# Rotating a batch of images by 180 degrees: the first store's lead strip in five transfers instead of one

## The chip, the cores and the metric

The kernel runs on one core of one Trainium2 chip. The metric is the time of one execution on the device in microseconds (us); a smaller number is better. Three executions of the kernel before gave 121.90, 121.97 and 122.13 us, median 121.97.

## The reference

The input is 32 x 3 images of 256 x 256 float32 values, 25.2 MB. Each image is turned by 180 degrees, which reverses its 65536 values when it is read as one row:

```python
def setup_inputs():
    batch, c, h, w = 32, 3, 256, 256
    return {"x": np.random.randn(batch, c, h, w).astype(np.float32)}

def reference(x: np.ndarray) -> np.ndarray:
    return np.rot90(x, k=2, axes=(-2, -1)).astype(np.float32)
```

## The kernel before

Nothing is computed; data is moved and reversed. Each of the 96 images is cut into four quarters of E = 16384 values (64 KB). A quarter is one partition's row in SBUF. The 384 quarters are three groups of 128: A holds the even ones of the first 64 images (image quarters 0 and 2), Bt the odd ones of the same images, Ct all four quarters of the last 32 images. All three tiles are in SBUF at once.

Reversing an image is done in two parts. The order of the quarters is turned by the store: the destination access pattern walks an image's quarters backwards (`::-1` in `store`, lines 52 to 54), so a store of group A names 64 images with 2 quarters each, in reversed order. The values within a quarter are turned in place by VectorE (DVE): `swap` (lines 56 to 60) exchanges a block of up to J = 2048 columns at the left with its mirror block at the right, with three reversing copies through a scratch tile T. `turn` (lines 69 to 73) does this for a stretch of left columns; a whole tile takes four swaps of 2048, 12 copies.

The work stands in the program in this order:

- loads (lines 64 to 67): A on SP's DMA queue, Bt on ACT's queue, behind it in the source Ct on SP's queue. Line 65 is a small memset that delays Bt's load. SP's queue is q1 in the profile, ACT's is q10. All stores go out on SP's queue too. Each DMA is spread over the 16 DMA engines, and in each engine the transfers of one queue run in the order of their issue; the last thing that an engine does for a transfer is a 4-byte write to a semaphore, here called the completion write. The transfer has landed when all 16 counts are there.
- line 76 turns the outer three blocks of A (columns 0 to 6143 and their mirrors); line 77 stores the first LEAD = 256 columns of A, 1 KB of each of 128 partitions. This is the strip. It is final as soon as the first swap is done.
- line 78 turns part of Bt, line 79 the innermost block of A, line 80 stores the rest of A (columns 256 to 16383, 63 KB a partition), called A's big store.
- lines 81 and 82: the rest of Bt and its store; lines 83 and 84: Ct and its store.

The strip waits for A's first swap and A's load alone, so SP issues it early, long before A's big store, and it stands in q1 behind C's load, which is still running. DVE's instructions are kept in program order (line 47). SP's instructions stand in the order of the source, each with a wait for what it needs; at the end of the program SP waits for the semaphore of every DMA, four instructions of at most two conditions each, then drains and meets the other engines at a barrier. DMA semaphores are handed out in turn from eight.

Of the kernel before, what the change touches and what calls it, by code (L numbers as in the profile page):

```python
# [2 lines left out]

os.environ.setdefault("NEURON_RT_ULTRASERVER_MODE", "4")

# [4 lines left out]


@with_exitstack
def kernel(
    ctx: ExitStack,
    tc: tile.TileContext,
    x: bass.AP,
    out: bass.AP,
):
    nc = tc.nc  # L20
    P = 128

    B, C, H, W = x.shape
    L = H * W
    G = 32
    E = L // 4
    J = E // 8

    xr = x.rearrange("b c h w -> (b c) (h w)").rearrange(
        "m (s e) -> (m s) e", s=4)  # L30
    om = out.rearrange("b c h w -> (b c) (h w)").rearrange(
        "m (s e) -> m s e", s=4)
    rows = 2 * P
    x4 = [xr[0:rows:2], xr[1:rows:2], xr[rows:rows + P]]
    o4 = [om[0:2 * G, 1::2], om[0:2 * G, 0::2], om[2 * G:3 * G]]

    pool = ctx.enter_context(tc.tile_pool(name="slots", bufs=1))
    A = pool.tile([P, E], x.dtype, tag="A")
    Bt = pool.tile([P, E], x.dtype, tag="B")
    Ct = pool.tile([P, E], x.dtype, tag="C")  # L40
    T = pool.tile([P, J], x.dtype, tag="T")

    def back(t, lo, hi):
        return t[:, hi - 1:(lo - 1 if lo else None):-1]

    def copy(dst, src):
        tc.keep_in_program_order(nc.vector.tensor_copy(out=dst, in_=src))  # L47

    def load(t, g, lo, hi, queue=nc.sync):
        return queue.dma_start(out=t[:, lo:hi], in_=x4[g][:, lo:hi])  # L50

    def store(t, g, lo, hi):
        return nc.sync.dma_start(
            out=o4[g][:, ::-1, lo:hi], in_=t[:, lo:hi])

    def swap(t, lo, w):
        hi = E - lo - w
        copy(T[:, 0:w], back(t, hi, hi + w))
        copy(t[:, hi:hi + w], back(t, lo, lo + w))
        copy(t[:, lo:lo + w], T[:, 0:w])  # L60

    MID = 2560
    LEAD = 256
    load(A, 0, 0, E)
    nc.vector.memset(Bt[:, 0:256], 0.0)  # L65
    load(Bt, 1, 0, E, nc.scalar)
    load(Ct, 2, 0, E)

    def turn(t, lo, hi):
        while lo < hi:  # L70
            w = min(J, hi - lo)
            swap(t, lo, w)
            lo += w

    half = E // 2
    turn(A, 0, half - J)
    store(A, 0, 0, LEAD)
    turn(Bt, 0, MID)
    turn(A, half - J, half)
    store(A, 0, LEAD, E)  # L80
    turn(Bt, MID, half)
    store(Bt, 1, 0, E)
    turn(Ct, 0, half)
    store(Ct, 2, 0, E)


# [1 line left out]
_INS = ['x']  # L88
_OUTS = [((32, 3, 256, 256), 'float32')]


# [23 lines left out]
```

## Time and profile before

| | |
|---|---|
| median of three executions | 121.97 us (121.90 to 122.13) |
| the profiled execution's own time | 121.90 us |
| its span, first to last instruction | 120.12 us |
| A's load landed | 39.45 us |
| Bt's load landed | 44.28 us |
| C's load landed, on the first and the last DMA engine | 60.72 and 61.23 us |
| strip: issued, landed on the last engine | 43.25 and 61.60 us |
| A's big store: issued, landed | 59.76 and 80.62 us |
| Bt's store: issued, landed | 70.31 and 99.96 us |
| C's store: issued, landed | 85.45 and 119.33 us |
| DVE busy | 44.9 us, 40 instructions |

The profile is of one execution. Its times count from the first instruction. A DMA instruction of SP or ACT is only the issue, some 0.4 to 0.6 us; the data moves later, in packets, one for each row of a transfer (64 KB, 63 KB or 1 KB here) and one for each completion write. The trace has each packet's start, length, size and queue, not its DMA engine. An engine starts its next packet about 4 ns before the last one ends. GB/s and DMA share count a packet in the slice in which it starts, so short slices can show more than the engines can carry.

### The profile page before, as it was taken

The numbers are of one execution on the slowest core, as the hardware profiler recorded it, in microseconds if no ns is written. First come the engines' busy times: TensorE is split into PE (matmuls) and PEld (weight loads), VectorE is DVE, ScalarE is ACT, GpSimd is POOL, SyncE is SP. The second block draws the span as 40 slices with busy tenths as digits, with TensorE's granted clock in tenths as the row PEclk, the third lists the DMA queues.
The fourth block names the chain that finished last, engine by engine and source line by source line (L and its number), as shares of the span: only waits on it lengthen the run. The fifth ranks groups of instructions, "written<-read, shape, count | busy, mean of one in ns | idle before, by whom it ended". The sixth has DMA issues, their size and how long they took to land.

```text
span 120.1 us, 97 instructions
## 1 busy us (share of the span) xinstructions
DVE 44.9 (37%) x40; POOL 0.2 (0%) x4
## 2 busy tenths in 40 slices
DVE  0000000000000899999999999999400000000000
POOL 0000000000000000000000000000000000000000
DMA  9888988898889988998899777988898889888980
GB/s 349 349 349 371 677 349 349 349 698 349 349 349 633 415 349 349 546 502 349 349 387 687 344 344 344 687 349 349 349 698 349 349 349 698 349 349 349 677 371 0
DMA packets 1008, 50.33 MB, mean 419 GB/s; under 512 B 112, under 2 KB 240, under 8 KB 240
## 3 DMA queue, kind: packets, MB, share of 16 engines
q1 hardware_dynamic: 864, 41.94, 81.3%
q10 hardware_dynamic: 144, 8.39, 16.1%
HBM read 25.17 MB, written 25.17 MB: 419 GB/s over the span
## 4 chain that ended last, share of the span: by engine, by line
DVE 38%; DMA 32%; issue 1%
DMA A<-in_x_dram 32%; DVE T L47 13%; DVE Bt L47 9%; DVE A L47 8%; DVE Ct L47 8%
## 5 line engine op out<-in xcount | busy, mean ns | idle before, releaser
L47 DVE COPY T<-A 128x2048 f32<-128x2048 f32 x4 | 4.9, 1226 | 38.4 <-DMA A<-in_x_dram 38.3
L47 DVE COPY T<-Bt 128x2048 f32<-128x2048 f32 (+2 forms) x5 | 5.1, 1014 | 0.2
L47 DVE COPY Bt<-T 128x2048 f32<-128x2048 f32 (+2 forms) x5 | 5.1, 1014 | 0.2
L47 DVE COPY Bt<-Bt 128x2048 f32<-128x2048 f32 (+2 forms) x5 | 5.1, 1013 | 0.2
L47 DVE COPY T<-Ct 128x2048 f32<-128x2048 f32 x4 | 4.9, 1227 | 0.1
L47 DVE COPY Ct<-T 128x2048 f32<-128x2048 f32 x4 | 4.9, 1227 | 0.1
L47 DVE COPY A<-T 128x2048 f32<-128x2048 f32 x4 | 4.9, 1227 | 0.1
L47 DVE COPY A<-A 128x2048 f32<-128x2048 f32 x4 | 4.9, 1227 | 0.1
L47 DVE COPY Ct<-Ct 128x2048 f32<-128x2048 f32 x4 | 4.9, 1226 | 0.1
L65 DVE MEMSET Bt<- 128x256 f32 x1 | 0.3, 272 | 0.9 <-PEq L99 0.9
L99 POOL MEMSET const-bfloat16-1.0<- 128x1 bf16 x1 | 0.1, 102 | 0.0
L99 POOL MEMSET const-uint8-127<- 128x1 uint8 x1 | 0.1, 102 | 0.0
L99 POOL MEMSET const-float32-0.0<- 128x1 f32 x1 | 0.1, 99 | 0.2 <-issue 0.2
L99 POOL MEMSET const-float32-1.0<- 128x1 f32 x1 | 0.1, 99 | 0.0
## 6 DMA issues: line engine op xcount, KB each, us to landing
out_dram<-A SPq DMA_DIRECT2D x1, 8064.0 KB, 20.9
out_dram<-A SPq DMA_DIRECT2D x1, 128.0 KB, 18.4
A<-in_x_dram SPq DMA_DIRECT2D x1, 38.7
Bt<-in_x_dram ACTq DMA_DIRECT2D x1, 43.1
Ct<-in_x_dram SPq DMA_DIRECT2D x1, 60.1
out_dram<-Bt SPq DMA_DIRECT2D x1, 29.6
out_dram<-Ct SPq DMA_DIRECT2D x1, 33.9
```

The source lines that it names most:

```text
L47: tc.keep_in_program_order(nc.vector.tensor_copy(out=dst, in_=src))
L65: nc.vector.memset(Bt[:, 0:256], 0.0)
L99: nc = _bacc.Bacc("TRN2", target_bir_lowering=False, num_devices=1)
```

## The change

The strip, one DMA of 64 images (128 rows of 1 KB), becomes five DMAs over the same columns, of 15, 14, 13, 12 and 10 images, 64 in all: 30, 28, 26, 24 and 20 rows of 1 KB from as many partitions. All five are issued by SP at the same place in the program. Nothing else in the source is touched; the lines behind it move down by four, so that line 110 is line 114 in the kernel after.

```diff
     half = E // 2
     turn(A, 0, half - J)
-    store(A, 0, 0, LEAD)
+    lo = 0
+    for n in (15, 14, 13, 12, 10):
+        nc.sync.dma_start(out=o4[0][lo:lo + n, ::-1, 0:LEAD],
+                          in_=A[2 * lo:2 * (lo + n), 0:LEAD])
+        lo += n
     turn(Bt, 0, MID)
     turn(A, half - J, half)
     store(A, 0, LEAD, E)
```

In the order in which the built program stands, SP has four more DMA instructions; only the first of the five waits (for A's load and the first three copies of DVE), and A's big store waits for DVE as before. The other engines' instructions stand as they did. The program has eleven DMAs instead of seven, so that three of the eight DMA semaphores are used twice: A's big store takes that of A's load, Bt's store that of Bt's load, C's store that of C's load. SP's four closing waits were, in order: the strip; A's big store; Bt's store; C's store. They become: the first two of the five; the third and C's store; the fourth and Bt's store; the fifth and A's big store.

## The prediction

> **What bounds the kernel now.** I read the page first, then the windows, then SP's timeline and waits, then the DMA view cut to the microsecond around 61, with the trace's packet records behind it (start, length, bytes and queue of each packet; not which of the 16 DMA engines moved it).
>
> From the page: span, the two digit rows, the two DMA queues.
>
> ```profile
> span 120.1 us, 97 instructions
> ...
> DVE  0000000000000899999999999999400000000000
> ...
> DMA  9888988898889988998899777988898889888980
> GB/s 349 349 349 371 677 349 349 349 698 349 349 349 633 415 349 349 546 502 349 349 387 687 344 344 344 687 349 349 349 698 349 349 349 698 349 349 349 677 371 0
> ...
> q1 hardware_dynamic: 864, 41.94, 81.3%
> q10 hardware_dynamic: 144, 8.39, 16.1%
> ```
>
> The DMA engines are busy from the second slice to the next to last (a packet counts where it starts, hence the uneven GB/s); together the queues fill 97.4% of 16 engines' span. DVE is off from slice 29 on. So the time is what 50.33 MB take on 16 full engines, plus start and close. In the records 64 KB packets take 2418 to 2420 ns in the load phase on every engine, 27.1 GB/s each, and no packet is shorter. A window over the last stores shows the same ceiling (us, DVE, POOL, clock, DMA share, GB/s):
>
> ```profile
> 80.00:118.70 38.70, 5.28 (x5) 0.00 (x0) 1.00 1.00 434
> ```
>
> The share is 1.00, so nothing can be caught up after 61 us: what an engine is late there, it is late at the end. SP's part, from the timeline and the waits:
>
> ```profile
> 43.25 17.06 SPq L53 DMA_DIRECT2D out_dram<-A  x2
> 70.31 0.54 SPq L53 DMA_DIRECT2D out_dram<-Bt  x1
> 85.45 0.54 SPq L53 DMA_DIRECT2D out_dram<-Ct  x1
> ```
>
> ```profile
> SPq L53 <- DVE A L47: 19.6, 2, 15.9
> SPq L110 <- DMA out_dram<-Ct: 19.3, 1, 19.3
> ```
>
> The first row merges the strip (issued at 43.25) and A's big store (43.25 + 17.06 - 0.55 = 59.76); between them SP waits 15.9 us for DVE. The last wait is for C's store, which starts and ends the close.
>
> The strip matters at one place only: it stands in q1 behind C's load and ahead of A's big store. Three cuts of the DMA view, 60.65 to 60.96, 60.96 to 61.00 and 61.00 to 61.21 us:
>
> ```profile
> DMA packets 82, 0.07 MB, mean 222 GB/s; under 512 B 15, under 2 KB 82, under 8 KB 82
> ```
>
> ```profile
> DMA packets 16, 0.46 MB, mean 11494 GB/s; under 512 B 1, under 2 KB 9, under 8 KB 9
> ```
>
> ```profile
> DMA packets 34, 0.60 MB, mean 2848 GB/s; under 512 B 8, under 2 KB 25, under 8 KB 25
> ```
>
> In the first nothing large starts; in the second 16 - 9 = 7 large packets start within 20 ns (60.972 to 60.992); in the third the other 9, the last at 61.201. So A's big store reaches the engines at about 60.975, 1.21 us after its issue. Engines that have done their strip by then (the earliest at 60.663) stand idle for up to 0.31 us; the late ones go straight on.
>
> **Row prices.** From the packet records: a 1 KB row takes 46 ns and the next starts after 42; from the last row's start to the completion write 44; from that to the next packet 6. An engine's strip now: 6 + 7 x 42 + 44 + 6 = 350 ns, and 60.851 (last completion of C's load) + 0.350 = 61.201, the record. A completion write to HBM stalls nothing.
>
> **The change, part by part.**
>
> 1. Issues. SP gets four more DMAs at 43.25. At 0.55 to 0.63 us each, five end by 46.4, 13 us ahead of A's store, and behind them stands only that store, which waits for DVE until 59.74. No engine's order changes and no new wait stands in front of a store. Cover gone: 2 to 2.5 us. In the engines the strip's issue shows: the packets that began around 43.4 to 43.9 average 2422 ns against 2418. Four more times 4 ns: **+0.02 us**.
>
> 2. Rows. I take it that a transfer of n images (2n rows) runs on n engines, two rows each, always the first n. An engine in j transfers then needs 6 + 92j ns (two rows 42 + 44, and 6 for the completion): j = 5 on ten engines, 466 (+116); j = 4 on two, 374 (+24); j = 3, 2, 1, 0 on one each: -68, -160, -252, -344. The trace does not show this split. If rows spread evenly anyway it is +32 ns at most for four more completions; if each transfer ran on one engine, that is the last rival. [...]
>
> 3. What the split does to the latest start. C's load ends on the engines at 60.318, .359, .426, .461, .474, .552, .585, .626, .700, .714, .746, .767, .772, .780, .824 and .851. Start of the big store = the later of 60.975 and end + 6 + 92j. Best matching (the four relieved engines are the four latest): .767 + .374 and .714 + .466 lead to 61.18 at the latest, -0.02. Worst (the latest is one of the ten): 61.317, **+0.116**. Even the best gains little, because eight engines are late and four are relieved. Middle: +0.05.
>
> 4. Where rows are read. Today every transfer cuts the 128 partitions into the same 16 shares, so an engine always works on its own. With 30, 28, 26, 24 and 20 partitions the shares shift: an engine reads rows that lie in another's share, which reads them at full rate for A's big store from 60.975. Every packet is pinned at 27.1 GB/s; whether that ceiling belongs to the engine or to the place in SBUF, the trace can't tell, since the two were never parted. Bounds: nothing (42 ns a row), or turns (84 ns). By turns: the engine of 60.851 has three rows done at 60.975 and seven to go, 7 x 42 = +0.29 on its +0.116, together +0.41; under the best matching .714 has four and a half to go: 61.18 + 0.19 = 61.37, +0.17. I take turns, at **+0.27**: a ceiling that is the same on all engines and never exceeded has no slack to lend. [...]
>
> 5. The close. SP ends by waiting for each DMA's semaphore. There are eight; with eleven DMAs three are used twice, and the built order of SP's closing waits becomes strip, **C's store**, B's store, A's store. Before, C's was the last; now two satisfied waits follow it. Rows: two such waits stand 60 ns apart at 86.03; from the last one at 119.35 to the next instruction it is 70 ns. Two more: 0.12 to 0.14, **+0.13 us**, on the path with no cover.
>
> Sum: 0.02 + 0.27 + 0.13 = +0.42. Passed on to the end in full or nearly: starts spread 0.23 us at 61, last packets 0.18 at 118.98. I take +0.40. The profiled execution took 121.90 (span 120.12 and 1.78 around it), so 122.30; the median 121.97 is 0.07 above it: 122.37, rounded **122.35**.
>
> **Rivals.**
> - *The ceiling is the engine's* (reads elsewhere cost nothing): 0.02 + 0.05 + 0.13 = +0.20, 122.17; for it speaks that loads (writing SBUF) and stores show nearly one packet time, against it nothing. It straddles what a measurement of this kernel can tell from no change, about 0.2% or 0.24 us.
> - *Levelling wins*, not slower: in the timed executions one of the relieved engines is far behind. One first packet does start late (2.724 against 1.744 us). Place: 61.2; price: such an engine gets at most 0.344 back, less 0.15 for items 1 and 5, so -0.19, 121.78; it decides once the last engine outside the four is ahead of the latest by more than what it is loaded with (0.02 to 0.12) and that 0.15. Against: here it is at most 0.084 ahead (.767 to .851). For more than 0.2% the store packets (2420 to 2434) must also fall to their floor.
> - *Rows don't spread as said*, or SP stands at a full queue: each transfer on one engine is 128 x 42 = 5.4 us, some +4 to +5 us, 126 to 127. The 16 shares of today's transfers speak against it.
>
> **Chances.** Turns 0.47 (0.42 slower by over 0.2%, 0.05 within); engine's ceiling 0.37 (0.12 slower, 0.25 within); levelling 0.09 (0.06 faster, 0.03 within); spread otherwise 0.07 (slower). Together faster 0.06, same 0.33, slower 0.61. Range: from the engine's ceiling with the best matching (0.02 - 0.02 + 0.13 = +0.13), less 0.2 for the scatter of the runs (0.23 between them): 121.9, to the worst matching by turns (0.02 + 0.41 + 0.13 = +0.56), and 0.17 for the scatter: 122.7. Left out: the last rival and most of the levelling.
>
> **What would show it.** Item 1: five SP issues ending by 46.5, A's store still at 59.76. Item 2: 128 rows of 1 KB and 64 completion writes for the strip (15 + 14 + 13 + 12 + 10). Items 3 and 4: the 1 KB rows near 61 at 46 ns or at twice that, and the last large start at 61.2 to 61.3 or 61.4 to 61.6; large packets in that slice longer than 2424. Item 5: two more waits between the last landing and the drains. The prediction is wrong if rows stay at 46 ns while the last start moves, or if the last landing moves by less than 0.05 us.

## The result, and the profile after

The changed kernel takes 122.18 us (median of 22 executions, 122.04 to 122.39) against 122.02 (22 executions, 121.82 to 122.34): a ratio of 1.0014, 95% interval 1.0007 to 1.0020. It is slower by some 0.16 us, less than half of the forecast +0.40, and within the 0.2% that the prediction called hard to tell from no change; the many executions resolve it. Beside the experiments below it was measured once more, at 122.22 against 122.02 us: 1.0021 (1.0011 to 1.0031).

The page after, span and queues:

```profile
span 120.3 us, 101 instructions
...
DMA packets 1056, 50.33 MB, mean 418 GB/s; under 512 B 160, under 2 KB 288, under 8 KB 288
## 3 DMA queue, kind: packets, MB, share of 16 engines
q1 hardware_dynamic: 912, 41.94, 81.3%
q10 hardware_dynamic: 144, 8.39, 16.1%
```

The bytes are the same. The 48 new packets are all under 512 bytes: 64 completion writes for the strip instead of 16, by the semaphores' records 15, 14, 13, 12 and 10 for its five transfers, read here as one from each engine that takes part. DVE's 44.9 us are unchanged. SP's timeline and waits after, and behind them a wait of before that the prediction does not show:

```profile
43.23 4.45 SPq L79 DMA_DIRECT2D out_dram<-A  x5
59.75 0.61 SPq L53 DMA_DIRECT2D out_dram<-A  x1
```

```profile
SPq L114 <- DMA out_dram<-Ct: 33.3, 1, 33.3
...
SPq L53 <- DVE A L47: 12.0, 1, 12.0
```

```profile
SPq L110 <- DMA out_dram<-Bt: 13.8, 1, 13.8
```

The five issues take 4.45 us, 0.77 to 1.02 each, and are over 12.0 us before A's big store, which is issued where it was. The wait for C's store was 19.3 us long and came behind one of 13.8 for Bt's store. Now it is 33.3, the two in one: SP comes to it at 86.09 and stands there until the end, and the waits for Bt's and A's stores come after it. The order of the closing waits is read from SP's instruction records, which the views leave out. There the last landing is at 119.365 (119.330 before); the wait ends at 119.39, two more start at 119.42 and 119.48, the first drain at 119.55 (119.42 before). The span is 0.16 us longer: 0.035 up to the last landing, 0.10 between landing and drain (0.09 became 0.19), 0.02 in the barrier behind it.

The seam at 61 us, where the engines go from loads to stores, in the DMA view cut from 60.96 to 61.00 and from 61.21 to 61.31 us:

```profile
DMA packets 16, 0.01 MB, mean 333 GB/s; under 512 B 3, under 2 KB 16, under 8 KB 16
```

```profile
DMA packets 12, 0.26 MB, mean 2622 GB/s; under 512 B 4, under 2 KB 8, under 8 KB 8
```

Where seven large packets started before, none does now; four start behind 61.21, the last at 61.304 (61.201 before). All 128 rows of 1 KB are 46 ns long, as before. Something not forecast stands ahead of them: 13 of the 16 last load packets of C took 2450 ns or more, up to 2793 (2420 to 2429 before), so that the early engines reached the strip 0.2 to 0.3 us later.

### The profile page after: what moved, and what is told of

It reads as the page before. It is cut to its first block, busy times and chain, and to the rows that moved or that the text cites. A ratio compares the mean times of both kernels' runs of the same rounds, so it can differ in the third digit from the quotient of the medians.

```text
span 120.3 us, 101 instructions
## 1 busy us (share of the span) xinstructions
DVE 44.9 (37%) x40; POOL 0.2 (0%) x4
## 4 chain that ended last, share of the span: by engine, by line
DVE 37%; DMA 32%; issue 1%
DMA A<-in_x_dram 32%; DVE T L47 12%; DVE Bt L47 9%; DVE A L47 8%; DVE Ct L47 8%
```

## The experiments

Two theories were put against each other. **The close**: nearly all of the loss is the two waits behind C's store. **The strip**: the uneven rows make the last start at 61 us later, and that is carried to the end. Beside them two questions of the prediction were open: whom the ceiling of 27.1 GB/s belongs to, and what an engine pays that reads another's share. The records show 128 rows and 16 completion writes in each transfer of 128 partitions, but neither the engine nor the partition of a packet; whose share a row lies in is the prediction's inference, here as there.

Each diff is cut to the lines that matter.

**close_only.** The strip stays one transfer; four copies of 4 bytes on ACT's queue, into a small tile D that is declared with the others, bring the DMAs to eleven.

```diff
     store(A, 0, 0, LEAD)
+    for i in range(4):
+        nc.scalar.dma_start(out=D[:, i:i + 1], in_=A[0:1, i:i + 1])
```

> One strip of 64 images as before; behind it four copies of 4 bytes from A into a small tile, on ACT's queue, so that the program has eleven DMAs and SP's closing waits take the order of the kernel after (C's store second of four). Theory of the close (the two waits behind C's store are nearly the whole loss): +0.13 us over the kernel before, two more waits between the last landing and the drains. Rival, theory of the strip (the later starts of A's big store at 61 us are carried to the end): 0 to +0.03 us.

122.07 against 121.92 us, 1.0015 (1.0007 to 1.0024): as much as the change itself, with the strip untouched. Landing to drain is 0.19 us. The time alone does not say which part of the kernel it comes from: in the profiled execution, which took 122.25 us, the last landing is also 0.21 us later than in the first profile of the kernel before.

**two_copies.** The same with two copies, nine DMAs.

> The control for the first experiment: one strip as before and two copies of 4 bytes instead of four, so nine DMAs, with C's store back in the last of SP's closing waits. Theory of the close: 0 to +0.04 us over the kernel before, some 0.11 less than with four copies. Rival (it is the small copies, or the strip, and not the close): no less than with four copies, +0.15 us.

122.03 against 122.02, 1.0002 (0.9993 to 1.0010), landing to drain 0.06 us. Two copies cost nothing that these runs can measure. The step to close_only is the order of the closing waits, and two copies more; the two ratios were measured in different sets of runs, and their intervals overlap a little (1.0007 to 1.0010). The times thus agree with the theory of the close without proving it. The traces are firmer: over all profiles, landing to drain is 0.06 to 0.09 us where no wait stands behind the one for C's store, 0.13 where one does (four_even and four_4k) and 0.19 where two do (the kernel after in both its profiles, and close_only). So the close gives 0.10 to 0.13 us of the loss.

**three_graded.** Nearly the same grading, and C's store is in the last of the closing waits. The diff is against the kernel after.

```diff
-    for n in (15, 14, 13, 12, 10):
+    for n in (28, 26, 10):
```

> The strip graded nearly as in the change, but in three transfers of 28, 26 and 10 images: 10 rows on ten engines, 8 on three, 4 on one, none on two. With nine DMAs C's store is in the last of SP's closing waits again. Theory of the close: 0 to +0.05 us over the kernel before. Theory of the strip: +0.10 to +0.16 us, as in the change.

122.03 against 121.92, 1.0009 (1.0001 to 1.0018), landing to drain 0.06. +0.11 us lies in the range of the strip's theory, not in that of the close's (0 to 0.05), though the interval, 0.01 to 0.22 us, reaches into both. So a graded strip without the late waits may still cost something; this is the part that these runs size badly.

**four_even.** Four transfers of 16 images; every engine keeps eight rows. The diff is against the kernel after.

```diff
-    for n in (15, 14, 13, 12, 10):
+    for n in (16, 16, 16, 16):
```

> The strip in four transfers of 16 images each, two rows on each of 16 engines, so that every engine has eight rows as before; ten DMAs, and C's store is in the last but one of SP's closing waits. Theory of the close: +0.06 to +0.08 us. Theory of the strip (uneven rows cost): 0 to +0.03 us. Beside it: if C's last load packets are stretched (over 2450 ns, as in the kernel after) because an engine reads rows of another's share, they are here too, since 32 partitions are cut otherwise than 128.

122.11 against 121.92, 1.0012 (1.0003 to 1.0020); landing to drain 0.13 us, between 0.06 to 0.09 and 0.19 as one late wait should give. The time is above both forecasts (+0.15 us by the ratio, interval 0.04 to 0.24, which reaches into the forecast of the close). Nothing shows that even rows are cheaper than graded ones. C's last load packets are lengthened here too (14 over 2450).

**two_columns.** Two transfers of 128 columns, all 128 partitions in both (by the inferred shares every engine in its own), good order at the close.

```diff
-    store(A, 0, 0, LEAD)
+    store(A, 0, 0, LEAD // 2)
+    store(A, 0, LEAD // 2, LEAD)
```

> The strip in two transfers of 128 columns each, all 64 images in both: 16 rows of 512 bytes on every engine, all of its own share, 18 queued items against 15 in the change; eight DMAs, C's store in the last of SP's closing waits. Time: 0 to +0.1 us by any theory (two rows of 512 bytes for one of 1 KB). Beside it: if the stretch of C's last load packets comes from other shares, none here is over 2440 ns; if it comes from many small rows queued, some are over 2450 ns.

122.06 against 121.92, 1.0009 (1.0000 to 1.0018). All 16 last load packets are lengthened, 2492 to 2736 ns. So that lengthening needs no other cut of the partitions, and by the inferred shares no reads from another's. It needs no more small rows than before either, as close_only showed 2596 to 2731 with eight rows of 1 KB.

**b_half_partitions** and **b_half_columns.** Whom the ceiling belongs to, at full size:

```diff
-    store(Bt, 1, 0, E)
+    for lo in (0, 32):
+        nc.sync.dma_start(out=o4[1][lo:lo + 32, ::-1],
+                          in_=Bt[2 * lo:2 * lo + 64, :])
```

```diff
-    store(Bt, 1, 0, E)
+    store(Bt, 1, 0, E // 2)
+    store(Bt, 1, E // 2, E)
```

> The disputed rule at full size: Bt's store (8 MB) in two transfers of 32 images, 64 partitions each, four rows of 64 KB on each of 16 engines. If the ceiling of 27.1 GB/s belongs to places in SBUF that each serve eight partitions, 64 partitions reach half of them: packets of 4800 ns, and the store takes some 38 us instead of 19.3, +19 us. If it belongs to the engine: packets of 2420 ns, 0 to +0.1 us.

> The control: Bt's store in two transfers of all 64 images, half of the columns each (rows of 32 KB), so that every engine keeps its share. 0 to +0.1 us by both theories, packets of 1210 ns.

144.07 us by partitions, 122.14 by columns (one execution each, before 121.92). Windows from 80.7 to 99 us, all in Bt's store, by partitions and then by columns (us, DVE, POOL, clock, DMA share, GB/s):

```profile
80.70:99.00 18.30, 4.76 (x4) 0.00 (x0) 1.00 0.84 172
```

```profile
80.70:99.00 18.30, 4.73 (x4) 0.00 (x0) 1.00 1.00 430
```

By partitions the engines move two fifths of the bytes (a packet counts where it starts, which also makes the share 0.84; the packet records give just under half). In those records 16 packets run at a time, so all engines are busy, and 64 KB take 5108 ns instead of 2418, 2.11 times as long. Eight packets an engine of 2690 ns more are 21.5 us, nearly the whole difference. So the ceiling is not the engine's: the same 16 engines get half as much out of 64 partitions as out of 128. The cut also halves the stretch of DRAM that one transfer writes, from 16 to 8 MB. C's store writes 8 MB as well, out of 128 partitions, at 2418 to 2434 ns a packet in the kernel before. That speaks against DRAM and for the place in SBUF, though no run changes DRAM alone. How many partitions share one place, and which engines met there, no run shows.

**one_4k** and **four_4k.** The strip enlarged to LEAD = 1024, once in one transfer and once in four of 16 images (the loop of four_even). The line that both change:

```diff
-    LEAD = 256
+    LEAD = 1024
```

> LEAD is 1024 instead of 256: one strip of 4 KB rows, and A's big store is smaller by as much. Control for the next. The bytes are the same and every engine reads its own share: -0.1 to +0.1 us. 4 KB rows of some 155 ns.

> LEAD is 1024 and the strip goes out in four transfers of 16 images: 32 partitions at a time on 16 engines, eight rows of 4 KB on each engine in all, read out of other engines' shares. Two engines that stand at one place at once were seen to halve in Bt's store by half of the partitions (5108 against 2418 ns for 64 KB). If the strip pays that price in full, the eight rows take 2.4 us instead of 1.2 and the last start of A's big store moves by +1 us or more, and the time with it. If engines that come one after the other seldom meet at a place: rows of 155 ns and +0.07 to +0.2 us (close and completions).

122.82 and 122.77 against 122.02: 1.0063 (1.0051 to 1.0075) and 1.0065 (1.0053 to 1.0077). Rows cut in four transfers of 32 partitions, in other shares by the inference, cost nothing against those of one transfer even at 4 KB: all 128 rows are 159 ns long in both. So the full price of turns is refuted for the strip. Both kernels missed their forecasts: the control by 0.7 us, and four_4k, at +0.75, lies between its two. The control's DMA view from 60.3 to 61.3 us, and behind it that of the kernel before:

```profile
DMA packets 0, 0.00 MB, mean 0 GB/s; under 512 B 0, under 2 KB 0, under 8 KB 0
```

```profile
DMA packets 176, 1.16 MB, mean 1163 GB/s; under 512 B 32, under 2 KB 160, under 8 KB 160
```

With the larger strip nothing starts in that microsecond. C's last load packets, begun around 58 us, take 3093 to 3580 ns there (mean 3370), and everything behind them is late by that. The rows of the strip and all of A's big store (2267 ns each, 128 of 128) are then all of one length.

The records of four_4k also speak for engines that do meet. The first load packet ends there at 61.04 us, and four rows with their two completion writes take 0.63; if each engine has two rows of each transfer, as eight rows and four completion writes an engine suggest, none has left the first two transfers, which are 64 partitions, up to 61.67. At 61.66 us 15 rows are under way, 4 KB in 159 ns each (the next row starts after 155): some 390 GB/s, where Bt's store got some 205 out of 64 partitions (16 packets of 64 KB in 5.11 us).

**one_2k.** LEAD = 512, to see whether the lengthening follows the bytes.

> LEAD is 512: one strip of 2 KB rows. With 4 KB rows all of C's last load packets were 950 ns longer on all engines, and the time 0.77 us more. Theory of reading ahead (rows of the strip that an engine reads from SBUF while it still writes its last load packet there hold that packet up, byte for byte: 32 KB an engine give up to 1.2 us, 8 KB up to 0.3): 16 KB give 0.35 to 0.6 us on the last load packets, and +0.25 to +0.45 us of time. Rival (it is the 4 KB size or chance): none, -0.05 to +0.1 us.

122.38 against 122.06, 1.0027 (1.0005 to 1.0049), with five executions between 121.92 and 122.62; the profiled one took 121.97. Its last load packets are 2456 to 2816 ns, mean 2641, +221 on 2420 where 350 to 600 were expected. The time, +0.33 us with an interval of 0.06 to 0.60, fits the theory of reading ahead but does not exclude the rival; the packets of the profiled execution fall short of the theory.

**before_again.** A second profile of the kernel before.

> The kernel before, a second profile. If the lengthening of C's last load packets (0 to 9 ns in the first profile, mean 131 ns in the changed kernel's) belongs to the change, there is none here; if it comes and goes from execution to execution, or hangs on the small transfers, some engines may show 50 to 250 ns. Time as before, 121.8 to 122.3 us.

121.92 us; 11 of its 16 last load packets are over 2450 ns (2428 to 2636, mean 2508). So the lengthening at 1 KB is not the change's alone: it comes and goes with the execution. It may still be larger with the change. The mean is 4 to 88 ns over 2420 in the five profiles with the strip as before and at most two copies beside it (both of the kernel before, two_copies, both halves of Bt's store); it is 135 and 127 in the two of the kernel after, 112 to 204 in three_graded, four_even and two_columns, and 253 in close_only. With one profile of most kernels this is a hint and no proof. The last of the 16 first packets of A's big store starts at 61.358 here and at 61.201 in the first profile.

**change_again.** The changed kernel's second profile.

> The changed kernel once more, beside the others on one chip. Both theories: +0.12 to +0.2 us over the kernel before; between the last landing and the first drain 0.19 us against 0.09 in the kernel before; all 1 KB rows at 46 ns.

122.22 against 122.02 us, the top of what both theories allowed. Landing to drain 0.19 us, rows 46 ns, last start 61.465 (61.304 in the first profile).

## Why the prediction was right and where it was wrong

Sign and range held. The size did not: the sum was +0.42, the measured loss +0.16. The case that it thought likeliest, turns, did not come, and the loss, 0.14%, stayed within the 0.2% to which it had given a chance of 0.33. Its own signs of being wrong came true in the first pair of profiles: the rows stayed at 46 ns while the last start moved by 0.10 us, and the last landing moved by 0.035, less than 0.05. The time lies in the range because the range begins at the sum of the rival. By its steps:

1. Issues: hidden, as said. Their duration was underrated (0.77 to 1.02 us each, not 0.55 to 0.63; 47.7 us, not 46.4), with 12.0 us of cover left. The +0.02 us in the engines can't be told from the scatter.
2. Rows: 64 completion writes, 15, 14, 13, 12 and 10 of the semaphores' counts coming with the data. The number of engines in each transfer, counted by these writes, is the one taken. The split behind +0.116 and +0.05, two rows an engine and always the same first ones, was the author's assumption, and no run shows it by itself. What the trace of the kernel after shows: the 64 writes can be joined in 16 chains with steps of 90 to 92 ns, each starting at a completion write of C's load, as two rows of 42 and 44 ns would have it. Ten chains of five, two of four and one each of three, two, one and none fit, as taken; other sharings fit too.
3. The last start moved by +0.10 us in the first pair of profiles (61.201 to 61.304) and by +0.11 in the second (61.358 to 61.465), inside the -0.02 to +0.116 that was worked out. But two executions of one kernel differ by 0.16 there. Counted from A's landing, the last start is at 21.73 to 21.88 us in the five profiles with the strip as before, and at 21.87 and 21.89 in the two of the kernel after: at the upper end of the scatter, so that a shift by the grading is possible and not shown. Of the first pair's +0.10 us 0.035 was left at the last landing; the second pair's landing moved by 0.20 (119.35 to 119.55). That starts are passed on nearly in full was not shown.
4. **The failed step is the +0.27 us for rows read out of other shares**, of which 0.05 is the start of step 3 and some 0.22 the price of turns. (The middle of its two bounds, +0.17 and +0.41, would be +0.29.) The reason was half right: the ceiling is not the engine's, at 5108 against 2418 ns from half of the partitions. That two engines take turns at one place, at 84 ns a row, was the author's estimate from the 42 ns, and no run shows it. The price was wrong: no row of the strip was longer than 46 ns, nor any of 4 KB longer than 159 ns, and four transfers of 4 KB rows cost no more than one. Why the small rows escape a ceiling that halves a whole store is not settled. That the engines seldom meet does not explain it: in four_4k, with two rows of each transfer on each engine, 15 rows were under way out of 64 partitions at once, at some 390 GB/s, about twice the 205 that Bt's store got out of as many. The rows may be read ahead while the last load packet is still being written, which would hide their wait in that packet. But that packet was lengthened less in four transfers than in one (710 against 950 ns), and no run tests reading ahead by itself.
5. The close: the order, and that it lies on the path, were right; 0.10 us to the first drain, and 0.02 in the barrier behind it in the first profile, against 0.13. The times of close_only and two_copies, 1.0015 and 1.0002, agree with it.

Without the price of turns the sum is +0.20 us, 122.17: the rival of the engine's ceiling named the measured time, though its premise, that the ceiling is the engine's, is what the halves of Bt's store refuted. That it came so close is in part luck: its +0.05 us for the starts is not shown, and the kernel before now took 122.02, not the 121.97 that it started from. Levelling did not win: no graded strip was faster than the kernel before. What stays open is how the rest of the loss, some 0.03 to 0.1 us, divides between the grading, the added transfers, the longer last load packets and the scatter at 61 us. three_graded, four_even and two_columns, each with some of these, all lie 0.1 to 0.15 us above the kernel before by their ratios, with intervals as wide as that.

No version here is faster than the kernel before.

## What to carry to other kernels

Splitting a DMA added more than packets here: it used up semaphores and changed in which order the program's end waits for its stores, and each wait that came behind the last landing added some 0.05 to 0.06 us (landing to drain 0.06 to 0.09 us without one, 0.13 with one, 0.19 with two); count the DMAs and read the closing waits of the built program. The DMA engines were busy from end to end (97.4% of 16 engines' span), and a levelling worked out at -0.02 to +0.116 us was smaller than the scatter of the last start between two executions of one kernel, 0.16 us. So check in a second profile of the unchanged kernel that the unevenness is there at all. The limit measured at full size (64 KB packets of 5108 ns out of 64 partitions, 2418 before) was no price for the strip, whose rows stayed at 46 ns (1 KB) and 159 ns (4 KB): measure it at the size in question.

## What the runs showed that was not expected

- At the switch from loads to stores, the last load packets of the engines took longer than 2420 ns: by 950 ns in the mean with a strip of 32 KB an engine in one transfer, 710 in four, 221 with 16 KB, 4 to 253 with 8 KB; each of the larger sizes has one profile. With 32 KB the kernel took up to 0.77 us longer. That the strip's rows are read ahead from SBUF against the load's writing there would fit the largest size; it wasn't tested apart, and no run leaves the strip out.
- SP took longer to issue the DMAs with fewer than 16 completion writes: 0.77 to 1.04 us with 10 to 15 (both profiles of the kernel after), 0.59 to 0.68 for the four even transfers with 16.
- The 4-byte copies on ACT's queue in close_only landed at 51.31, 56.21, 61.33 and 61.72 us: the first three about 5 us apart, which is the time of two 64 KB packets of the other queue (4.84 us), for one small copy and its completion write.
